# Low parts of the queries on 128 rows instead of 64, in the scores of three attentions

## Chip, core and metric

One Trainium2 chip, one NeuronCore. The metric is the device time of one execution in microseconds, as the median of the runs. Of the engines, TensorE (PE in the profile) multiplies matrices and loads their weights (PEld), VectorE (DVE) and ScalarE (ACT) read its results from PSUM, GpSimd (POOL) works on SBUF, and SyncE (SP) issues most DMAs.

## What is computed

A block of two layers: an input projection, four attentions side by side, a gated merge of their outputs, an output projection, and a mixture of 16 experts. The change touches the scores of three attentions: one with a sliding window and shared key heads (`win`), one that subtracts two softmaxes (`dif`), and one over a neighbourhood (`nat`). In all three, 64 numbers per head are multiplied; the fourth (`mla`) has 96.

```
def dense_attention(q, k, v):
    scale = q.shape[-1] ** -0.5

    def block(qb):
        logits = jnp.einsum('bqhd,bkhd->bhqk', qb, k).astype(jnp.float32) * scale
        p = jax.nn.softmax(logits, axis=-1)
        return jnp.einsum('bhqk,bkhd->bqhd', p.astype(v.dtype), v)
...
def trunk_layer(...):
    ys = [
        window_attention(wq, wk, wv, wkc, wvc, win_sink),
        dif_out(diff_attention(dq, jnp.concatenate([dkc, dk], axis=1), jnp.concatenate([dvc, dv], axis=1), lam)),
        neighbourhood_attention(nq, nk, nv, nkc, nvc, nat_rpb),
        flat_heads(dense_attention(mq, jnp.concatenate([mkc, mk], axis=1), jnp.concatenate([mvc, mv], axis=1))),
    ]
```

256 tokens and 256 context tokens make four tiles of 128. In layer 0 all four tiles are queries, in layer 1 only the first two.

## The kernel before

Products that need full precision are made of two fp32r parts each: a high part (`whi`, `hT[0]`) and what is left, a low part (`wlo`, `hT[1]`). A projection then takes three products (`mm3`, lines 284 to 288: high by high, high by low, low by high); ACT makes each high part and DVE the low part of the streamed weights (`parts`, lines 273 to 275).

**Scores.** A unit is a pair of heads and a tile of 128 queries. A head has 64 numbers, so a pair fills the 128 rows of a tile of queries or keys. The keys of a head i are kept in one 128-row tile: the high part on the head's own 64 rows, the low part on the other head's rows (`qk_post`, line 761). `heads` (line 911) makes the query side: `qs[i]` has the query's high part on both halves of the rows, so one 128-row product gives high by high plus high by low. ACT copies it (line 917), POOL repeats it on the other half (`QX`, recorded at line 261), and POOL subtracts to get the low part (line 919), which stands on the head's own 64 rows of one tile `ql` that both heads share. The second product of a head takes only these 64 rows of `ql` and of the keys. So a unit has four score products: two with 128 rows and two with 64. All are issued in `softmax2` (line 773), into the score banks `S0` and `S1`, which have one buffer each; with 512 columns for the first two query tiles and 256 for the others. Behind them come on DVE the maximum (line 782), on ACT the exponential (line 787), on POOL the normalization (line 261, `pp`), on TensorE the transposes (line 281), and the product with V (lines 827, 870).

**Tiles.** `qp` (line 765) takes the next of three buffers (`BUFS["qp"]`) of four 128x128 quarters: `qs[0]`, `qs[1]`, `ql`, and one that is unused. Every unit takes a new one. The `mla` attention takes its query parts from the same buffers, all four quarters.

**Order.** Within a layer the stages run one after the other (`run_main`): the projections of one attention go as main steps, and the units of the attention before as `side` items between them; so `win` runs beside the projections for `dif`, `dif` beside a merge, `mla` beside another, `nat` beside the merge of `mla`. `drain` ends each stage. The program is written in that order, and a scheduler with its own estimate of times sets the sequence of PE, DVE, ACT and POOL from it; SP's DMAs keep the written order. In the trace `win` stands at 97 to 225 us and 1233 to 1291, `dif` at 229 to 338 and 1318 to 1376, `nat` at 588 to 696 and 1544 to 1610. Then come the output projection and the experts, whose weights are streamed from about 700 to 1230 us and from 1612 us on.

Of the kernel before, what the change touches and what calls it, by code (L numbers as in the profile page):

```python
# [210 lines left out]
def kernel(ctx: ExitStack, tc: tile.TileContext, a, out, dbg=None, depth=L):  # L211
# [470 lines left out]
    def attention_layer(l, T, hT):  # L682
# [225 lines left out]
                act(nats[key, t], ps, AF.Copy)  # L908
            return f

        def heads(q, k):

            *qs, ql, _ = qp()
            rows = [slice(i * 64, (i + 1) * 64) for i in range(2)]
            for i in range(2):
                r, x = rows[i], rows[1 - i]
                act(qs[i][r], q[r], AF.Copy)  # L917
                QX(qs[i][x], qs[i][r])
                G.tensor_tensor(ql[r], q[r], qs[i][r], op=OP.subtract)
            return [[(i, qs[i], k[i], True, False) for i in range(2)],  # L920
                    [(i, ql[rows[i]], k[i][rows[i]], False, True) for i in range(2)]]

        def stage_win():
            w = {}
            idl = ids["wkv"]

            def ev_kv(t, ps):
                if "V" not in w:
                    kvt = b8r("wkv")
                    w["V"] = gp.tile([P, 512], F32, name="wV", tag="wV").rearrange("p (t n) -> p t n", t=4)  # L930
                    w["kT"] = [kvt[:, 0:512], kvt[:, 512:1024]]
                nats["wk", t] = t2("nat")
                act(nats["wk", t][:, :P], ps[:, :P], AF.Copy)
                V.tensor_copy(w["V"][:, t, :], ps[:, P:2 * P])
                if t == 3:
                    posts.extend(qk_post({t: nats["wk", t] for t in AT}, AT, 2, "wkn", *w["kT"]))

            def kv(t):

                ps = acc()  # L940
                tok = slice(t * P, (t + 1) * P)
                for n in range(KT):
                    mm3(ps[:, :256], (hT[0][:, n, tok], hT[1][:, n, tok]), ws.hl(*idl[n], ahead=t == 3), n == 0, n == KT - 1)
                ev_kv(t, ps)

            def ev_q(t, ps):
                n = t2("nat")
                act(n.rearrange("p (c s d) -> p s c d", c=4, s=2), ps.rearrange("p (s c d) -> p s c d", c=4, s=2), AF.Copy)
                nats["wq", t] = n
                if t == QT[-1]:  # L950
                    w["qT"] = b8("wqT")
                    posts.extend(qk_post({t: nats["wq", t] for t in QT}, QT, 8, "wqn", w["qT"]))
            steps = steps0(ev_kv, ev_q) if l == 0 else [lambda t=t: kv(t) for t in AT] + proj_steps("wq", 512, QT, ev_q)

            def slots():
                def ops(pi, tok, ks):
                    return heads(w["qT"].rearrange("p (b n) -> p b n", b=4)[:, pi, tok], [v[:, ks] for v in w["kT"]])
                return std_slots(ops, lambda b, pi, i: w["V"][:, b, i * 64:(i + 1) * 64], y_of(0), range(4), sink=True, mask=True)
            return steps, slots

        def stage_qkv(pre, gq, gk, br):
# [19 lines left out]

            def ops(pi, tok, ks):
                return heads(w["qT"].rearrange("p (b n) -> p b n", b=4)[:, pi, tok],
                             [v.rearrange("p (b n) -> p b n", b=4)[:, pi, ks] for v in w["kT"]])
            if br == 1:
                return steps, lambda: dif_slots(ops, w["V"], y_of(1))
            bias_t = {}

            def bias_load(pi):
# [14 lines left out]
                return r  # L1004

            def slots():
                bias_load(0)
                return std_slots(ops, lambda b, pi, i: w["V"][:, b, (2 * pi + i) * 64:(2 * pi + i + 1) * 64], y_of(2), range(4), bias=bias)
            return steps, slots
# [1182 lines left out]
```

## Time and profile before

| | |
|---|---|
| median of 3 runs | 1977.82 us (1973.92 to 1977.86) |
| profiled execution | 1979.95 us |
| its span in the trace | 1977.9 us |
| granted TensorE clock, mean | 0.957 of full speed |
| busy: PE, DVE, ACT, POOL | 92%, 61%, 51%, 37% |

An engine's busy time is no measure of how well it is used: products are pipelined, so that each is drawn longer than the distance to the next. What a product costs is read from the distance between starts in the order of time. A row of the order of time gives start, length, engine, line, operation, output and inputs, and then the shape of the weights (rows*columns) and of the moving data; in square brackets stands how long the engine was idle before and what ended that. Neighbours of one kind are merged under "xcount", and then the first one's shape is shown. "issue" means that nothing that the profile shows was waited for.

### The profile page before, as it was taken

To read this page: it belongs to the slowest core of one execution; us is meant where nothing else is said; L and a number is where in the kernel's file an instruction comes from. 1 tells how busy PE (TensorE), PEld (TensorE's weight loads), DVE (VectorE), ACT (ScalarE), POOL (GpSimd) and SP (SyncE) were. 2 spreads that over 40 slices of the span, in tenths; PEclk is the share of its full clock that TensorE was granted. 3 is DMA by queue.
4 is the path that set the end of the run, shared out by engine and by line. 5 is a ranking of instruction groups with operands and counts; after the bars stand their busy time and mean duration, and the time that the engine had idled before them with its cause. 6 is when DMAs were issued, how large, how long until landed. Compare 5 with 4: busy or idle time off the path is not lost. (4 is left out here: it accounts for less than half of the span.)

```text
span 1977.9 us, 26705 instructions
## 1 busy us (share of the span) xinstructions
PE 1825.4 (92%) x8748; PEld 1252.3 (63%) x8748; DVE 1215.9 (61%) x2314; ACT 1010.0 (51%) x2201; POOL 725.6 (37%) x1066
## 2 busy tenths in 40 slices
PE   7989999999999999849998959999999999699998
PEld 5846678777666678635554538566877667555563
DVE  4657566566555545765564456766668777656664
ACT  4436465554545534436555435655545655555451
POOL 0657353444535510352222234643336630111110
PEclk9989999999999999969999969899999999799999
DMA  9331052211481245648999855336422365379995
GB/s 341 130 138 33 27 179 64 62 54 51 174 316 56 75 162 207 226 169 305 390 395 396 348 211 208 129 123 233 126 69 89 107 212 215 129 303 419 420 400 243
DMA packets 120875, 392.39 MB, mean 198 GB/s; under 512 B 12652, under 2 KB 30348, under 8 KB 93968
## 3 DMA queue, kind: packets, MB, share of 16 engines
q1 hardware_dynamic: 114832, 377.36, 52.2%
q0 software_dynamic: 3424, 8.08, 1.2%
q10 hardware_dynamic: 2464, 5.08, 0.7%
q8 instruction: 73, 1.20, 0.2%
q14 instruction: 82, 0.67, 0.1%
HBM read 379.19 MB, written 15.27 MB: 199 GB/s over the span
## 5 line engine op out<-in xcount | busy, mean ns | idle before, releaser
L287 PE MATMUL acc<-wlo,hT 128*128 128x512 f32 (+2 forms) x976 | 384.7, 394 | 1.8 <-DVE wlo L275 1.8
L288 PE MATMUL acc<-whi,hT 128*128 128x512 f32 (+2 forms) x976 | 378.7, 390 | 0.2 <-DVE hT L275 0.2
L286 PE MATMUL acc<-whi,hT 128*128 128x512 f32 (+2 forms) x976 | 363.9, 398 | 2.3 <-ACT nat L1016 1.1
L274 ACT ACTIVATE whi<-raw 128x512 fp32r<-128x512 f32 (+1 forms) x376 | 231.5, 625 | 250.6 <-PE acc L288 184.1
L275 DVE TENSOR_TENSOR wlo<-raw,whi 128x512 fp32r<-128x512 f32 (+1 forms) x376 | 274.9, 742 | 137.2 <-ACT whi L274 135.7
L312 DVE TENSOR_TENSOR wlo<-raw,whi 128x512 fp32r<-128x512 f32 x256 | 189.6, 784 | 79.8 <-ACT whi L308 79.4
L308 ACT ACTIVATE whi<-raw 128x512 fp32r<-128x512 f32 x304 | 182.1, 628 | 80.1 <-PE h L288 43.2
L286 PEld LDWEIGHTS acc<-whi,hT 128*128 128x128 f32 x976 | 182.4, 188 | 56.0 <-issue 11.5
L287 PEld LDWEIGHTS acc<-wlo,hT 128*128 128x128 f32 x976 | 183.9, 188 | 46.0 <-issue 8.7
L288 PEld LDWEIGHTS acc<-whi,hT 128*128 128x128 f32 x976 | 183.5, 188 | 39.4 <-issue 5.8
L261 POOL TENSOR_SCALAR pp<-pp,sml 128x512 f32<-128x512 f32 (+1 forms) x168 | 120.0, 723 | 145.2 <-DVE sml L792 89.6
L787 ACT ACTIVATE pp<-S,sml 128x512 f32<-128x512 f32 (+1 forms) x192 | 117.3, 613 | 87.5 <-DVE sml L782 56.3
L310 POOL TENSOR_TENSOR wlo<-raw,whi 128x512 fp32r<-128x512 f32 x48 | 63.4, 1322 | 242.2 <-ACT whi L308 173.2
L782 DVE TENSOR_REDUCE sml<-S 128x1 f32<-128x512 f32 (+1 forms) x192 | 113.0, 597 | 43.6 <-PE S L773 41.9
L619 POOL TENSOR_TENSOR sml<-sml,nhalf 128x1 f32<-128x1 f32 (+3 forms) x110 | 122.7, 1117 | 7.0
L1966 PE MATMUL hh<-raw,xh 128*64 128x512 f32 x344 | 115.4, 614 | 5.0 <-DMA raw<-in_moe_w_dram 5.0
L287 PE MATMUL h<-wlo,xe 128*128 128x512 f32 x256 | 106.6, 416 | 2.1 <-POOL wlo L310 0.8
L618 POOL TENSOR_SCALAR sml<-sml 128x1 f32<-128x1 f32 (+3 forms) x110 | 37.5, 340 | 189.0 <-DVE sml L713 111.4
L281 PE MATMUL T<-cst,pp 128*128 128x128 f32 x560 | 92.2, 288 | 12.5 <-POOL pp L261 8.9
L286 PE MATMUL h<-whi,xe 128*128 128x512 f32 x256 | 100.3, 399 | 1.6 <-PEq L1612 1.6
L288 PE MATMUL h<-whi,xe 128*128 128x512 f32 x256 | 101.3, 396 | 0.0
L261 POOL TENSOR_SCALAR qp<-qp 64x128 fp32r<-64x128 f32 x144 | 53.4, 371 | 120.8 <-ACT qp L917 103.5
(440 smaller groups left out, 3449.7 us busy)
## 6 DMA issues: line engine op xcount, KB each, us to landing
raw<-in_moe_w_dram SPq DMA_DIRECT2D x133, 1024.0 KB
raw<-in_w_in_dram SPq DMA_DIRECT2D x124, 512.0 KB
raw<-in_ada_w_dram SPq DMA_DIRECT2D x48, 1024.0 KB
w<-in_moe_w_dram SPq DMA_DIRECT2D x36, 1024.0 KB
w<-in_moe_w_dram SPq DMA_DIRECT2D x60, 256.0 KB
raw<-in_w_branch_dram SPq DMA_DIRECT2D x24, 512.0 KB
raw<-in_w_out_dram SPq DMA_DIRECT2D x24, 512.0 KB
w<-in_moe_w_dram SPq DMA_DIRECT2D x16, 512.0 KB
```

Source lines behind the costliest of these rows:

```text
L261: G.tensor_scalar(o, i, s, s2, op0=OP.mult, op1=OP.mult)
L274: act(hi, src, AF.Copy)
L275: V.tensor_tensor(lo, src, hi, op=OP.subtract)
L286: mm(o, s[0], whl[0], start=start, stop=False)
L287: mm(o, s[0], whl[1], start=False, stop=False)
L288: mm(o, s[1], whl[0], start=False, stop=stop)
L308: act(hi, raw, AF.Copy)
L312: V.tensor_tensor(lo, raw, hi, op=OP.subtract)
L619: G.tensor_tensor(r, r, nhalf[:, :n], op=OP.pow)
L782: V.tensor_reduce(nm[:, i:i + 1], ps[i][:, :nk], axis=AX.X, op=OP.max, negate=True)
L787: act(p[:, :nk], ps[i][:, :nk], AF.Exp, bias=nm[:, i:i + 1], accum_out=nm[:, 2 + i:3 + i])
L1966: mm(hh[r:r + 64], x, wm.cols(pi, kk * 512, 512), start=k == 0, stop=k == KT - 1, tile_position=(0, r))
```

## The change

The unused fourth quarter of a query tile becomes a second low tile, so that each head has one. `padded` is called once at the start of each of the three attentions; it takes the three buffers and lets DVE write zeros (a constant times 0) on those rows of the two low tiles that belong to the other head. `heads` takes the three in turn for the units; POOL writes a low part on its own 64 rows, and the other rows stay zero. The second product of each head then takes all 128 rows of its low tile and of the keys: the zeros meet the keys' low part. The lines of the products in `softmax2` are the same.

```
+        def padded():
+
+            ring = [qp() for _ in range(BUFS["qp"])]
+            for v in ring:
+                for i in range(2):
+                    V.tensor_scalar(v[2 + i][64 - i * 64:128 - i * 64], C("ident")[64 - i * 64:128 - i * 64], 0.0, None, op0=OP.mult)
+            return ring
+
+        def heads(q, k, ring):
+
+
+            *qs, l0, l1 = ring[0]
+            ring.append(ring.pop(0))
+            ql = (l0, l1)
             for i in range(2):
-                r, x = rows[i], rows[1 - i]
+                r, x = slice(i * 64, i * 64 + 64), slice(64 - i * 64, 128 - i * 64)
                 act(qs[i][r], q[r], AF.Copy)
                 QX(qs[i][x], qs[i][r])
-                G.tensor_tensor(ql[r], q[r], qs[i][r], op=OP.subtract)
-            return [[(i, qs[i], k[i], True, False) for i in range(2)],
-                    [(i, ql[rows[i]], k[i][rows[i]], False, True) for i in range(2)]]
+                G.tensor_tensor(ql[i][r], q[r], qs[i][r], op=OP.subtract)
+            return [[(i, v[i], k[i], g == 0, g == 1) for i in range(2)] for g, v in enumerate((qs, ql))]
...
             def slots():
+                ring = padded()
+
                 def ops(pi, tok, ks):
...
             if br == 1:
-                return steps, lambda: dif_slots(ops, w["V"], y_of(1))
+                def dif():
+                    w["ring"] = padded()
+                    return dif_slots(ops, w["V"], y_of(1))
+                return steps, dif
...
             def slots():
+                w["ring"] = padded()
                 bias_load(0)
```

How the built programs stand: TensorE, ACT and POOL have as many instructions as before, DVE has 36 more. On TensorE, the first score of `nat` in layer 0 (beside the merge of `mla`) stood so before; `x2` is a head's high and low product, `hT` the projections' input, and L539 belongs to another small product:

```order
L286 MATMUL acc<-whi,hT 128x512
L287 MATMUL acc<-wlo,hT 128x512
L288 MATMUL acc<-whi,hT 128x512
L773 MATMUL S_5896<-nkT,qp 128x512 x2
L539 MATMUL S_5598<-raw,cs_89 32x512 x4
L286 MATMUL acc<-whi,hT 128x512
L287 MATMUL acc<-wlo,hT 128x512
```

and stands so now:

```order
L288 MATMUL acc<-whi,hT 128x512
L539 MATMUL S_5584<-raw,cs_89 32x512 x4
L773 MATMUL S_5890<-nkT,qp 128x512 x2
L286 MATMUL acc<-whi,hT 128x512
L287 MATMUL acc<-wlo,hT 128x512
L288 MATMUL acc<-whi,hT 128x512
```

A head's two products are still one behind the other between the products of the merge; only the small product beside them has changed sides.

On DVE, where `dif` begins in layer 0 (L782, L785, L790 and L792 belong to the softmax of the last `win` units, L275 splits streamed weights), it was before:

```order
L790 TENSOR_TENSOR sml<-sml 128x1
L782 TENSOR_REDUCE sml<-S_2166 128x1
L785 TENSOR_TENSOR sml<-sml,nsink 128x1
L790 TENSOR_TENSOR sml<-sml 128x1
L792 RECIPROCAL sml<-sml 128x2
L275 TENSOR_TENSOR wlo<-raw,whi 128x512 x2
L782 TENSOR_REDUCE sml<-S_2299 128x1
```

and is now, with the fills of two of the three query tiles (the first tile's stand some rows earlier):

```order
L782 TENSOR_REDUCE sml<-S_2087 128x1
L916 TENSOR_SCALAR qp<-cst 64x128 x2
L785 TENSOR_TENSOR sml<-sml,nsink 128x1 x2
L275 TENSOR_TENSOR wlo<-raw,whi 128x512
...
L782 TENSOR_REDUCE sml<-S_2159 128x1
L785 TENSOR_TENSOR sml<-sml,nsink 128x1
L916 TENSOR_SCALAR qp<-cst 64x128 x2
L785 TENSOR_TENSOR sml<-sml,nsink 128x1
L790 TENSOR_TENSOR sml<-sml 128x1
```

The fills (L916) stand two at a time between the last softmaxes of `win`, each behind a reduction of a `win` score.

## Rows read from the trace of the kernel before

**Rows 1.** The page: busy time of each engine.
```profile
PE 1825.4 (92%) x8748; PEld 1252.3 (63%) x8748; DVE 1215.9 (61%) x2314; ACT 1010.0 (51%) x2201; POOL 725.6 (37%) x1066
```

**Rows 2.** Busy by stretch: from:to, length, engines (instructions), clock, DMA, GB/s; seven summed.
```profile
125.00:167.00 42.00, 30.20 (x118) 17.45 (x119) 31.32 (x86) 28.77 (x86) 32.98 (x56) 0.72 0.05 15
...
1230.00:1253.00 23.00, 18.64 (x69) 10.93 (x71) 12.21 (x34) 14.63 (x39) 14.05 (x32) 0.78 0.01 2
1253.00:1293.00 40.00, 40.00 (x219) 24.09 (x212) 34.56 (x71) 21.92 (x53) 30.08 (x33) 1.00 0.50 184
...
sum 490.00, PE 483.64 PEld 325.63 DVE 310.60 ACT 257.28 POOL 243.94; mean PE 69.09 PEld 46.52 DVE 44.37 ACT 36.75 POOL 34.85
...
900.00:1230.00 330.00, 296.33 (x1370) 186.49 (x1369) 184.76 (x285) 174.05 (x327) 95.17 (x90) 0.93 0.85 328
```

**Rows 3.** Line 773: one attention's products, TensorE's idle time; products (x) by stretch.
```profile
L773 PE MATMUL S<-nkT,qp x96: 277/477/505, 588.4 to 1609.7; 128*128 128x512 f32 x32, 64*128 64x512 f32 x32, 128*128 128x256 f32 x16, 64*128 64x256 f32 x16
...
  issue: 38.1, 121
...
125.00:167.00 42.00, 15.69 (x32) 7.44 (x32) 0.72 0.05 15
...
227.00:340.00 113.00, 24.16 (x64) 12.03 (x64) 0.97 0.34 105
...
1230.00:1253.00 23.00, 9.46 (x16) 3.79 (x16) 0.78 0.01 2
```

**Rows 4.** Order of time, TensorE and its weight loader, around low products.
```profile
595.04 0.40 PE L286 MATMUL acc<-whi,hT 128*128 128x512 f32 x1
...
595.27 0.82 PE L773 MATMUL S<-nkT,qp 128*128 128x512 f32 x2
...
595.60 0.18 PEld L773 LDWEIGHTS S<-nkT,qp 64*128 64x128 f32 x1 [0.37 <-issue]
...
596.03 0.19 PEld L287 LDWEIGHTS acc<-wlo,hT 128*128 128x128 f32 x1 [0.24 <-issue]
...
596.36 0.40 PE L288 MATMUL acc<-whi,hT 128*128 128x512 f32 x1
...
607.01 0.59 PE L773 MATMUL S<-nkT,qp 128*128 128x256 f32 x2
...
607.86 0.39 PE L286 MATMUL acc<-whi,hT 128*128 128x512 f32 x1
...
622.71 0.91 PE L773 MATMUL S<-nkT,qp 128*128 128x512 f32 x3
...
623.12 0.19 PEld L773 LDWEIGHTS S<-nkT,qp 64*128 64x128 f32 x2 [0.25 <-issue]
...
623.55 0.66 PE L281 MATMUL T<-cst,pp 128*128 128x128 f32 x4
...
1375.61 0.19 PEld L773 LDWEIGHTS S<-dkT,qp 64*128 64x128 f32 x2 [0.37 <-issue]
```

**Rows 5.** Order of time, products of the fourth attention with 96 rows.
```profile
413.27 1.35 PEld L773 LDWEIGHTS S<-mkT,qp 96*128 96x128 f32 x6
...
413.51 1.55 PE L773 MATMUL S<-mkT,qp 96*128 96x512 f32 x6
...
414.90 0.27 PE L281 MATMUL T<-cst,pp 128*128 128x128 f32 x1
```

**Rows 6.** TensorE's waits in 125 to 167 (us, times, longest); then one score there.
```profile
PE T L281 <- POOL pp L261: 7.2, 3, 3.9
...
144.20 1.50 PE L773 MATMUL S<-wkv,qp 128*128 128x512 f32 x2
...
145.62 0.69 PE L827 MATMUL T<-pT,wV 128*64 128x256 f32 x2
```

**Rows 7.** DVE groups: multiplications by a constant (busy us, mean ns).
```profile
L1884 DVE TENSOR_SCALAR OHe<-cst,rkq 128x128 fp32r<-128x128 f32 x8 | 2.1, 327 | 0.0
...
L659 DVE TENSOR_SCALAR sm<-sm 128x128 f32<-128x128 f32 x2 | 0.5, 241 | 0.0
```

More of the change, by code (lines that the diff above doesn't have):

```diff
@@ L909, in nat_evac @@
             return f
-        def heads(q, k):
-            *qs, ql, _ = qp()
-            rows = [slice(i * 64, (i + 1) * 64) for i in range(2)]
+        def padded():
[8 more added lines that the diff above has]
+            ql = (l0, l1)
             for i in range(2):
-                r, x = rows[i], rows[1 - i]
+                r, x = slice(i * 64, i * 64 + 64), slice(64 - i * 64, 128 - i * 64)
                 act(qs[i][r], q[r], AF.Copy)
                 QX(qs[i][x], qs[i][r])
-                G.tensor_tensor(ql[r], q[r], qs[i][r], op=OP.subtract)
-            return [[(i, qs[i], k[i], True, False) for i in range(2)],
-                    [(i, ql[rows[i]], k[i][rows[i]], False, True) for i in range(2)]]
+                G.tensor_tensor(ql[i][r], q[r], qs[i][r], op=OP.subtract)
+            return [[(i, v[i], k[i], g == 0, g == 1) for i in range(2)] for g, v in enumerate((qs, ql))]
         def stage_win():
@@ L955, in slots @@
             def slots():
+                ring = padded()
                 def ops(pi, tok, ks):
-                    return heads(w["qT"].rearrange("p (b n) -> p b n", b=4)[:, pi, tok], [v[:, ks] for v in w["kT"]])
+                    return heads(w["qT"].rearrange("p (b n) -> p b n", b=4)[:, pi, tok], [v[:, ks] for v in w["kT"]], ring)
                 return std_slots(ops, lambda b, pi, i: w["V"][:, b, i * 64:(i + 1) * 64], y_of(0), range(4), sink=True, mask=True)
@@ L983, in ops @@
                 return heads(w["qT"].rearrange("p (b n) -> p b n", b=4)[:, pi, tok],
-                             [v.rearrange("p (b n) -> p b n", b=4)[:, pi, ks] for v in w["kT"]])
+                             [v.rearrange("p (b n) -> p b n", b=4)[:, pi, ks] for v in w["kT"]], w["ring"])
             if br == 1:
-                return steps, lambda: dif_slots(ops, w["V"], y_of(1))
+                def dif():
+                    w["ring"] = padded()
+                    return dif_slots(ops, w["V"], y_of(1))
+                return steps, dif
             bias_t = {}
```

## The prediction

> **What bounds the kernel now.** I read the page first, then busy time by stretch, then the score products of line 773 by stretch, and last single products in the order of time. On the page TensorE is busy 92% of the span, the next engine, DVE, 61% [rows 1]; these are averages over stages with different limits, so the stretches must tell. The three changed attentions stand in nine stretches. In seven of them (95 to 125, 167 to 227, 227 to 340, 585 to 700, 1253 to 1293, 1316 to 1378 and 1542 to 1612 us) TensorE is busy 483.6 of 490 us in sum, DVE 63% of it, ACT 53% and POOL 50%, and the closest that another engine comes is DVE with 86% in 1253 to 1293 [rows 2]. There TensorE sets the time. In the other two, 125 to 167 and 1230 to 1253, it is busy 48.8 of 65 us, at a mean granted clock of 0.72 and 0.78 (a part of the time at 1.2 GHz, not 2.4) [rows 2], and waits for POOL and ACT of the softmax [rows 6].
>
> The three attentions hold 288 score products in 72 units of four, half of them with 64 rows: 32 of each kind with 512 columns and 16 with 256 in `nat`, and as many in the other two. TensorE sat idle before line 773 for 38.1 us in 121 places until "issue", that is, behind nothing that the profile shows [rows 3]. The order of time shows where.
>
> **What a 64-row product costs.** Take the score at 595.27 us: the high product starts at 595.27, the weights of the product after the low one are taken at 596.03, and the product behind that starts at 596.36. That is 1.09 us from the first to the fourth start; 128-row products follow each other by 0.23 us (595.04, 595.27), so three take 0.69: 0.40 us too much. The weight loader shows why: it takes 128-row weights while the product before still runs, but stood 0.37 us before it took the 64-row weights, and 0.24 us before it took 128-row ones again [rows 4]. With 256 columns, 607.01 to 607.86 is 0.85 us, where 0.12 + 0.12 + 0.23 = 0.47 would do: 0.38 too much (0.12 is an estimate: half of 0.23 for half the columns) [rows 4]. That the rows make it, not the change between high and low parts nor the buffers, shows in a fourth attention that the change leaves alone: six 96-row products with weights from the same buffers stand between 128-row ones and take 413.51 to 414.90, 0.23 each, without a stop of the loader [rows 5]. I take **0.39 us** for a low product that stands alone.
>
> **The change, part by part.** (a) The 144 low products get 128 rows; their number, columns and sums stay. By the 96-row rows, each then costs its ordinary 0.23 or 0.12 us. 120 of them stand in the seven stretches and 24, half of 32 and 16, in the two others [rows 3]. In eight units, all in the seven stretches, both low products stand together; the first of these with 512 columns is at 623.12, the last at 1375.61. There they start as one, and three products take 622.71 to 623.55, 0.84 us instead of 0.69; a part of that comes from the transposes on either side, and I take 0.1 [rows 4]. So 104 x 0.39 + 8 x 0.1 = **41.4 us of TensorE time** where it sets the time. How much of it reaches the end: a unit's softmax on ACT, DVE and POOL gets up to 11% less time under it (in 227 to 340, 32 low products, 12.5 of 113 us) [rows 3]. TensorE's waits in these stretches are 6.4 us in all now, so the others deliver on time; DVE at 63% has room, at 86% little, but that is 40 of the 490 us [rows 2]. I take 90%, 37.3 us; the ends are half, 20.7, and all of it.
>
> (b) In the two starved stretches a low product is dearer: at 144.20 a high and a low one take 1.42 us at the lower clock, against 0.76 (595.27 to 596.03) at the higher [rows 4, 6], so the surplus lies between 0.39 and twice that. 24 x 0.39 to 0.78 = 9.4 to 18.7 us; I take 14. TensorE waits there for POOL and ACT, which wait for scores in turn, since each of the two score banks has one buffer: a part of the product's time is in that circle. I take half, **7 us**, between 0 and 14.
>
> (c) The zeros: 36 DVE fills of 64x128, six at each of six attention starts. No such form is in the trace; a 128x128 multiplication by a constant took 241 ns, one with fp32r output 327 ns [rows 7]: 8.7 to 11.8 us of DVE in all, at most 2 at a place. In the order they stand two at a time between reductions and the `wlo` splits that feed the projections; DVE's idle third hides them. A fill waits for the release of its buffer, but in the order its last reader comes before the reduction just ahead on DVE. I deduct **1 us**; uncovered it is 11.8.
>
> (d) The ring: before, each unit took the next of three tiles; now the same three are kept through an attention. The depth is the same, and a write waits for the readers of its quarter instead of the whole tile's. POOL and ACT run as many instructions as before. I cost this at nothing.
>
> (e) The scheduler's order: most of TensorE's sequence is the same; in layer 0 the second attention's scores and the last of the first's are mixed otherwise. No work is added; I give it nothing, and 5 us either way in the range.
>
> Sum: 37.3 + 7 - 1 = 43 us from the profiled execution's 1979.95 us, 1937. That execution is 2.1 us over the median of the runs, 1977.82, so I forecast **1935 us**. What follows the attentions moves with them: the expert weights, where DMA is at 85% between 900 and 1230 us [rows 2], are issued when the attention stages are drained, and so start earlier by as much.
>
> **The rivals.** *All of it comes back* (7%): both kinds of stretches in full, 41.4 + 14 = 55 us, 1922 us. For it, that TensorE waits so little now; against it, the waits on POOL and ACT in 125 to 167.
>
> *The softmax takes the place* (12%): with TensorE faster, transposes wait for POOL's normalized scores in the seven stretches too, as in 125 to 167, where three such waits took 7.2 us [rows 6]. Half of (a) and nothing of (b): 20 us, 1958. Against it: POOL and ACT have half of these stretches idle [rows 2].
>
> *Slower, by the fills* (3%): a fill holds DVE until the attention before has let go of its buffer, and with it the splits behind. A unit of `dif` takes 113 / 16 = 7.1 us (227 to 340); two units' wait at each of the four starts that follow another attention would be 57 us, 14 more than the gain: 1991. It turns the sign from 11 us a place. Against it: the place of the fills in the order, behind work that already needs those readers.
>
> *Slower, by lost concurrency* (2%): two 64-row products on different halves of the rows can run at the same time, and the eight units with both together show it. If every unit ran its two low products in the time of one, at no other price, 128 rows would add one product to each: 48 x 0.23 + 24 x 0.12 = 14 us [rows 3], 1992 us. It decides where low products stand together and the return is free; but 64 units have them apart, and even together three products take 0.84 us instead of 0.69 [rows 4]. The Trainium skill (TensorE: Matmul & The Clock Gate, Part 3 on packing small matmuls) speaks for this rival: a product with few rows takes as long as a full one, and pays when it is put beside another on distinct row groups, since they run together. By that rule the change loses the 14 us; the trace agrees on the common start, in eight units, and not on the price of one that stands alone.
>
> *It does not do what it says* (4%): the loader's stop comes from something else in these products and remains at 128 rows. Then only the fills are added: 1978 to 1981. Against it speak the 96-row products.
>
> **How the numbers follow.** The forecast has 72%, with a range of its own from 1924 (all of (a), 14 of (b)) to 1951 (two thirds of (a), none of (b)). The whole range, 1916 to 1960, takes in the first rival with the 5 us of (e) and the middle of the second; the second's far end, the slower ones and the last are left out, some 14%. A measurement of this kernel can tell about 0.2%, 4 us, from no change: faster has 72 + 7 + 12 = 91%, within it the last rival's 4%, slower 5%.
>
> **What would show it.** In the profile of the changed kernel: no 64-row form at line 773; idle time there until "issue" down from 38.1 us to a few; a score's products 0.23 us apart in 585 to 700; that attention (115 us now) shorter by 9 to 12 us. If the second rival holds, TensorE's share in the seven stretches falls, with waits on POOL or ACT `pp` before transposes. The forecast fails if low products of 128 rows still take over 0.3 us, if DVE waits some us before a fill, or if the expert stages end when they did before.

## The result, and the profile after

The changed kernel takes 1946.72 us (median of 4 runs, 1945.53 to 1947.77), the kernel before 1977.84 beside it: a ratio of 0.9842, with a 95% interval from 0.9829 to 0.9855. That is 31 us less where 43 were forecast. The profiled execution took 1947.77 us with a span of 1945.7; before, 1979.95 and 1977.9.

The page's line of busy times, in the form of [rows 1]:

```profile
PE 1782.1 (92%) x8748; PEld 1249.5 (64%) x8748; DVE 1224.5 (63%) x2350; ACT 1006.2 (52%) x2201; POOL 734.3 (38%) x1066
```

TensorE runs as many products as before, in 43.3 us less busy time. The share is 92% in both: it is still the engine that sets the time. DVE has 36 instructions more, the fills with zeros, and 8.6 us more busy time.

The products of line 773 for the third attention, with the idle time before that line, in the form of [rows 3]:

```profile
L773 PE MATMUL S<-nkT,qp x96: 278/393/505, 573.0 to 1574.2; 128*128 128x512 f32 x64, 128*128 128x256 f32 x32
...
  issue: 4.0, 7
```

No 64-row form is left, the median product went from 477 to 393 ns, and the stop behind "issue" went from 38.1 us in 121 places to 4.0 in 7. The heading of [rows 3] and the prediction call those 38.1 us TensorE's idle time; asked for each engine alone, the trace gives all of them to the weight loader (PEld) and none to the products. One score in the order of time (start, length, engine, line, operation), to be held against [rows 4]:

```profile
578.31 0.40 PE L286 MATMUL acc<-whi,hT 128*128 128x512 f32 x1
578.55 0.62 PE L773 MATMUL S<-nkT,qp 128*128 128x512 f32 x2
579.01 0.40 PE L287 MATMUL acc<-wlo,hT 128*128 128x512 f32 x1
579.25 0.39 PE L288 MATMUL acc<-whi,hT 128*128 128x512 f32 x1
```

The high and the low product and the next one behind them now take 0.70 us (578.55 to 579.25), 0.23 each, where three such starts took 1.09.

To see where the time went I cut both executions at the same products of the projections, so that each stretch holds the same work. In order: window and second attention of layer 0; the fourth attention; the third; the expert stage of layer 0; window, second, and fourth with third attention of layer 1; the last expert stage. Columns are from:to, length, busy time of TensorE, its loader, DVE, ACT and POOL (instructions), granted clock, DMA share, GB/s. First the kernel before:

```profile
114.10:335.10 221.00, 206.28 (x939) 144.33 (x938) 144.73 (x357) 125.23 (x352) 122.46 (x214) 0.92 0.24 73
335.10:564.20 229.10, 222.50 (x1124) 163.47 (x1123) 139.62 (x266) 115.36 (x284) 107.15 (x160) 1.00 0.32 108
590.10:697.70 107.60, 106.31 (x497) 73.62 (x493) 60.05 (x118) 54.41 (x139) 54.64 (x88) 1.00 0.22 64
800.40:1188.50 388.10, 322.07 (x1500) 198.47 (x1498) 222.37 (x374) 190.67 (x342) 122.65 (x132) 0.89 0.81 307
1215.60:1292.40 76.80, 72.44 (x349) 46.41 (x347) 56.92 (x119) 43.03 (x106) 52.84 (x72) 0.93 0.26 97
1315.80:1382.60 66.80, 66.80 (x327) 40.57 (x326) 41.87 (x89) 37.55 (x95) 27.16 (x50) 1.00 0.58 200
1510.90:1620.30 109.40, 105.09 (x511) 74.69 (x510) 85.52 (x144) 64.87 (x149) 61.45 (x83) 1.00 0.38 119
1676.70:1945.80 269.10, 243.39 (x1061) 146.32 (x1059) 165.48 (x285) 144.15 (x251) 43.94 (x37) 0.95 0.83 336
```

The changed kernel, the same stretches:

```profile
112.50:316.80 204.30, 184.93 (x939) 141.24 (x939) 144.17 (x361) 122.14 (x351) 121.92 (x210) 0.93 0.25 79
316.80:547.80 231.00, 223.38 (x1125) 163.79 (x1124) 141.20 (x272) 115.55 (x284) 107.82 (x163) 1.00 0.32 107
573.50:670.40 96.90, 95.30 (x493) 73.16 (x492) 58.39 (x116) 53.15 (x139) 58.03 (x89) 1.00 0.25 71
773.10:1160.50 387.40, 321.88 (x1500) 197.34 (x1498) 224.57 (x380) 191.41 (x342) 123.55 (x132) 0.90 0.81 307
1187.60:1263.40 75.80, 69.87 (x350) 46.72 (x348) 59.28 (x124) 42.72 (x106) 54.99 (x72) 0.95 0.27 98
1286.60:1349.10 62.50, 62.50 (x329) 41.41 (x328) 42.49 (x89) 37.25 (x95) 27.51 (x50) 1.00 0.67 213
1477.80:1584.50 106.70, 100.60 (x512) 75.01 (x510) 86.83 (x149) 64.68 (x149) 61.95 (x83) 1.00 0.39 120
1640.90:1912.80 271.90, 245.09 (x1060) 146.79 (x1060) 165.58 (x285) 144.23 (x251) 43.79 (x37) 0.94 0.82 333
```

The five stretches with the changed products became shorter by 16.7, 10.7, 1.0, 4.3 and 2.7 us, 35.4 in sum. Against that stand 1.9 more in the fourth attention, which the change does not touch, and 2.1 more in the two expert stages together. Where TensorE had hardly any idle time before, in the third attention of layer 0 and the second of layer 1, it has hardly any after (1.3 to 1.6 us, and none in both). In the others its idle time (length less busy time) grew: from 14.7 to 19.4 us in the first stretch, from 4.4 to 5.9 in the window attention of layer 1, from 4.3 to 6.1 in the stretch with the third attention of layer 1. Each table is one execution, and the stretches with a clock under 1.00 vary more than the others; the experiments show by how much.

### The profile page after: what moved, and what is told of

Same layout as the page of the kernel before. It is cut to its first block, busy times and chain, and to the rows that moved or that the text cites. A ratio compares the mean times of both kernels' runs of the same rounds, so it can differ in the third digit from the quotient of the medians.

```text
span 1945.7 us, 26785 instructions
## 1 busy us (share of the span) xinstructions
PE 1782.1 (92%) x8748; PEld 1249.5 (64%) x8748; DVE 1224.5 (63%) x2350; ACT 1006.2 (52%) x2201; POOL 734.3 (38%) x1066
## 5 line engine op out<-in xcount | busy, mean ns | idle before, releaser
L275 DVE TENSOR_TENSOR wlo<-raw,whi 128x512 fp32r<-128x512 f32 (+1 forms) x376 | 272.4, 735 | 132.5 <-ACT whi L274 128.3
L782 DVE TENSOR_REDUCE sml<-S 128x1 f32<-128x512 f32 (+1 forms) x192 | 111.6, 595 | 31.1 <-PE S L773 30.0
L281 PEld LDWEIGHTS T<-cst,pp 128*128 128x128 f32 x560 | 68.5, 145 | 39.2 <-POOL pp L261 12.8
```

The lines of the kernel that those rows point to most:

```text
L275: V.tensor_tensor(lo, src, hi, op=OP.subtract)
L281: tp(pt[:, k * P:(k + 1) * P], src[:, kt * P:(kt + 1) * P], ident)
```

## The experiments

My theory going in: a product of 64 rows between full-height ones costs some 0.39 us in all, for the stop of the weight loader on the way there and back. The change pays by taking that away and by nothing else. The rivals were the other tiles and the other order (the ring), the two heads' low products at the same time, and, for the missing 12 us, the softmax.

### The ring and its order alone

The changed kernel's ring and its two low tiles, without zeros, and with the low products on 64 rows:

```diff
-            for v in ring:
-                for i in range(2):
-                    V.tensor_scalar(v[2 + i][64 - i * 64:128 - i * 64], C("ident")[64 - i * 64:128 - i * 64], 0.0, None, op0=OP.mult)
...
-            return [[(i, v[i], k[i], g == 0, g == 1) for i in range(2)] for g, v in enumerate((qs, ql))]
+            rows = [slice(i * 64, (i + 1) * 64) for i in range(2)]
+            return [[(i, qs[i], k[i], True, False) for i in range(2)],
+                    [(i, ql[i][rows[i]], k[i][rows[i]], False, True) for i in range(2)]]
```

> The changed kernel with its three kept tiles and a low tile per head, but without the fills, and with low products on 64 rows as before. My theory (the 64-row products themselves cost TensorE 0.39 us each when they stand alone): the gain is gone, 1978 us, between 1970 and 1984, and idle time before the scores until issue is near 38 us again. Rival (the gain comes from keeping the tiles, from finer waits, or from the new order): about as the changed kernel, 1943 to 1952 us.

Measured: 1979.6 us (1974.47 to 1987.68), the kernel before 1975.51 on the same chip; ratio 1.0029, from 1.0005 to 1.0054. The gain is gone, so tiles and order do not make it. If anything the ring costs a little. The loader's idle time before line 773 until "issue" is back, 34.7 us in 112 places. Three stretches of its trace are needed below: the window and second attention of layer 0, the fourth attention of layer 0, and the fourth with the third of layer 1:

```profile
113.90:326.20 212.30, 200.40 (x939) 141.71 (x938) 145.22 (x357) 122.98 (x351) 121.30 (x212) 0.94 0.24 76
326.20:555.30 229.10, 222.49 (x1124) 163.51 (x1123) 139.31 (x266) 115.11 (x284) 107.20 (x160) 1.00 0.32 109
1502.90:1617.60 114.70, 106.41 (x511) 75.63 (x510) 85.94 (x144) 65.03 (x149) 59.40 (x83) 0.99 0.40 125
```

The first is 8.7 us shorter than in the kernel before, with the same rows in every product. So a difference of that size in this stretch, read from one execution each, does not tell what the rows are worth there.

### The rows alone

The kernel before with one line changed: the low product takes all 128 rows of the low tile that both heads share. Each head then also gets the other head's low part times the low part of the keys. There are no zeros and no ring.

```diff
-                    [(i, ql[rows[i]], k[i][rows[i]], False, True) for i in range(2)]]
+                    [(i, ql, k[i], False, True) for i in range(2)]]
```

> The kernel before with one edit: the low product takes all 128 rows of the shared low tile and of the keys, with no zeros, no fills, no ring. On the other head's rows it adds the low part of the other head's query times the low part of the keys, a product of two remainders. My theory: as the changed kernel, 1946 us, between 1940 and 1952; if the fills cost the 1 us that I gave them, 1945. Rival (ring and order make the gain): 1972 to 1980 us.

Measured: 1944.21 us (1942.21 to 1948.55), ratio 0.9836, from 0.9818 to 0.9855. The row count alone brings all that the change brings. Its time is 2.5 us under the changed kernel's, but the two were timed apart and their intervals overlap; so it is not shown to be faster or slower, and it needs less code. Two of its stretches, the fourth attention of layer 0 and the fourth with the third of layer 1, differ from the changed kernel's by about 2 us:

```profile
321.20:550.10 228.90, 222.31 (x1125) 163.59 (x1125) 139.80 (x267) 115.28 (x284) 108.17 (x163) 1.00 0.32 108
...
1484.60:1589.30 104.70, 100.25 (x510) 74.84 (x509) 84.98 (x142) 64.80 (x149) 61.48 (x83) 1.00 0.38 121
```

In the changed kernel these took 231.0 and 106.7 us, here 228.9 and 104.7. In the fourth attention of layer 0 the extra time goes with the zeros: the kernel with the window attention taken back, which has them too, shows 231.0, and the ring without zeros 229.1. In the other stretch the ring is not cleared: the kernel with the window attention taken back shows 106.9, but the ring without zeros, on 64 rows, took 114.7 us where the kernel before took 109.4.

What a fill does shows in the changed kernel. The group of the fills (busy us, mean ns, idle before them):

```profile
L916 DVE TENSOR_SCALAR qp<-cst 64x128 fp32r<-64x128 f32 x36 | 10.8, 301 | 1.9 <-PE yh L2031 1.2
```

and the third attention's start in layer 1, DVE and then TensorE in the order of time:

```profile
1511.13 0.68 DVE L782 TENSOR_REDUCE sml<-S 128x1 f32<-128x512 f32 x1
1511.85 0.86 DVE L916 TENSOR_SCALAR qp<-cst 64x128 fp32r<-64x128 f32 x2
1512.63 0.68 DVE L271 COPY pT<-T 128x512 f32<-128x512 f32 x1
```

```profile
1511.06 0.73 PE L773 MATMUL S<-nkT,qp 128*128 128x512 f32 x2
1513.36 0.87 PE L827 MATMUL T<-pT,mV 128*64 128x256 f32 x6 [1.56 <-DVE pT L271]
```

Two fills of 0.86 us together stand just ahead of the copy of `pT`, and TensorE waits 1.56 us for that copy. The copy starts 0.78 us after the fills do, so their own length is half of the wait. The wait at this product, 1.1 to 1.6 us, stands in the four kernels here that fill zeros for the third attention, and in none of the other eight. At this place the fills are not hidden.

### Two low products together

If two 64-row products run at the same time, it may be better to keep them and put each pair together. Both kernels here hold the first low product until both high ones have been issued; the second differs from the first in the low product's rows, as in the experiment before.

```diff
...
+                for p in prods[0]:
+                    ins = prod(*p)
+                for p in prods[1]:
+                    with tc.issue_after(ins.ins):
+                        ins = prod(*p)
...
```

> The kernel before, with the four products of a unit kept together on TensorE: high, high, low, low, and both low ones with 64 rows, so that they can run at the same time in all 72 units. My theory, from the units that had them together: a unit loses 0.1 to 0.17 us instead of twice 0.39, so 7 to 12 us over all against the same order with 128 rows, most of it on the path: 5 to 12 us slower than that one, and well under the kernel before, 1950 to 1965 us. Rival (concurrency, by the rule on packing): 14 us less TensorE time than the same order with 128 rows, so 8 to 14 us faster than that one.

> The same order, high, high, low, low, with 128 rows in the low products (shared low tile, no zeros, as in the kernel with one edit). My theory: near the changed kernel, 1944 to 1956 us, since holding the first low product until the second score bank is free costs a little latency only; 5 to 12 us faster than its 64-row twin. Rival (concurrency): 8 to 14 us slower than the twin.

Measured: 1980.75 us (1978.72 to 1982.8) on 64 rows, ratio 1.0026, from 1.0017 to 1.0036; 1969.63 us (1968.16 to 1971.75) on 128 rows, ratio 0.9968, from 0.9958 to 0.9979. In this order the full height is 11.1 us faster, as the theory had it, and not 8 to 14 slower as the concurrency rival had it. In the trace on 64 rows, 70 of the 72 units have their two low products one behind the other. The size has a simple reading: 72 units at 0.15 us (0.84 less 0.69, [rows 4]) make 10.8. By that reading the two run together, which saves one product's 0.23 us of the 0.39, and 0.16 remain to be paid.

Their own times missed what I expected of them: they lie 16 and 14 us over the upper end, and the one on 128 rows 25 us over the rows alone in the old order. In the second attention of layer 1, where TensorE never idles, one part of it can be read. The stretch for the rows alone, then the pairs on 128 and on 64 rows:

```profile
1293.30:1355.80 62.50, 62.50 (x328) 41.43 (x327) 42.54 (x89) 37.36 (x95) 26.79 (x50) 1.00 0.63 213
```

```profile
1306.60:1373.20 66.60, 66.26 (x328) 41.66 (x327) 42.69 (x87) 36.72 (x94) 24.62 (x50) 1.00 0.59 200
```

```profile
1311.00:1378.90 67.90, 67.90 (x328) 40.26 (x327) 41.66 (x87) 36.78 (x94) 25.22 (x50) 1.00 0.57 196
```

The same number of products takes 4.1 us longer in the held order, at the same rows. Line 539 issues narrow products of 32 columns of weights, in groups. In the order of time of the pairs on 128 rows, groups stand like this:

```profile
1316.82 1.07 PE L539 MATMUL acc<-raw,cs 128*32 128x512 f32 x8
...
1326.32 1.04 PE L539 MATMUL acc<-raw,cs 128*32 128x512 f32 x2
```

A group of two takes as long as a group of eight. In the held order there are 14 groups in this stretch, for the rows alone 11: three more at about 1 us each are 3 of the 4.1. So the hold lets other work fall apart into smaller groups. The stretch of the two pairs gives the price again: 67.9 against 66.6 us, 1.3 for eight units, 0.16 each. The rest of the 25 us I did not follow; cut in the same way, the traces of the held and of the old order on 128 rows differ in all the stretches with changed attentions (8.1 and 6.5 us in layer 0; 1.5, 4.1 and 5.7 in layer 1).

### The window attention on 64 rows, and it alone on 128

The changed kernel with the window attention taken back, by a copy of the old function beside the new one:

```diff
-                ring = padded()
-
...
-                    return heads(w["qT"].rearrange("p (b n) -> p b n", b=4)[:, pi, tok], [v[:, ks] for v in w["kT"]], ring)
+                    return heads64(w["qT"].rearrange("p (b n) -> p b n", b=4)[:, pi, tok], [v[:, ks] for v in w["kT"]])
```

> The changed kernel with one stage taken back: the 48 low products of the window attention (32 in layer 0, 16 in layer 1) use 64 rows again and carry no zeros; the other two attentions keep 128 rows. What it tells: what the window attention's share of the gain is. The prediction's own sum for these 48 (7 us in the two starved stretches, and 24 products at 90% of 0.39 us or less outside them) would make this kernel 13 to 15 us slower than the changed kernel, 1959 to 1962 us. My theory, from the stages of the two traces: the window attention waits for its softmax chain, so most of what its products save turns into waiting there. In layer 1 that stretch became 1.0 us shorter and no more; in layer 0 the window attention and the one after it became 16.7 us shorter together, of which some 11 belong to the 32 products of the other (as the third attention got 10.6 for its own 32). That leaves 5 or 6 plus 1: 1951 to 1955 us, 5 to 8 slower than the changed kernel. A rival, that the window attention brings nothing at all: 1946 to 1949.

Measured: 1953.28 us (1949.91 to 1956.25), ratio 0.9889, from 0.9865 to 0.9912. That is 6.6 us over the changed kernel, inside the 5 to 8 of the theory. The two were timed apart; held each against the kernel before timed beside it, the gains are 31.1 and 22.7 us, 8.4 apart. The counterpart is the kernel before with all rows in the window attention alone:

```diff
...
-                    [(i, ql[rows[i]], k[i][rows[i]], False, True) for i in range(2)]]
+                    [(i, ql, k[i], False, True) if full else (i, ql[rows[i]], k[i][rows[i]], False, True) for i in range(2)]]
```

> The kernel before with one edit, in the window attention alone: its 48 low products take all 128 rows of the shared low tile (so each head also gets the other head's low part times the low part of the keys); no zeros, no ring, and the other two attentions keep 64 rows. It is the counterpart of the kernel in which the window attention alone was taken back, without the ring of tiles. My theory says that the window attention is worth 5 to 8 us and not the 13 to 15 of the prediction's sum: 1967 to 1972 us where the kernel before takes 1975 to 1977. If the window attention were worth what the sum said, and the ring and the zeros had eaten it in the changed kernel: 1960 to 1963. If it is worth nothing: 1974 to 1978.

Measured: 1971.02 us (1969.63 to 1973.5), the kernel before 1976.14; ratio 0.9976, from 0.9965 to 0.9986, so 5.1 us, from 2.8 to 6.9. From both sides the window attention is worth 5 to 8 us, about half of what the prediction's sum gave it, and it is so without the ring too. In which layer it comes is not settled: against the kernel before, the second kernel is 5.9 us shorter in the first stretch (215.1 us) and 0.7 in the window attention of layer 1 (76.1); the first kernel is 1.1 longer than the changed one in the first stretch (205.4) and 4.2 in the other (80.0).

### A switch put where none was

The change cannot tell whether the price belongs to its three attentions or to any switch of row counts. In the fourth attention all products have 96 rows, and none stops the loader [rows 5]. Here its low products use 64 of them:

```diff
-                        r.append([(i, hi, k[0], True, False), (i, hi, k[1], False, False), (i, lo, k[0], False, True)])
+                        r.append([(i, hi, k[0], True, False), (i, hi, k[1], False, False), (i, lo[0:64], k[0][0:64], False, True)])
```

> The changed kernel with a switch of row counts added where neither kernel has one: the low product of each unit of the fourth attention uses 64 of its 96 rows (so 32 rows of 48 low products are left out of its scores), between products of 96 rows. The products become no longer and no shorter in columns; only the row count changes, three times in a unit of two banks. If the price is that of a switch from a full-height product to a 64-row one and back, it comes back here: 32 products over 512 columns at 0.39 us and 16 over 256 columns at 0.28 us make 17 us, and with the 72% that the change itself turned into time (31 of 43) 12: 1957 to 1966 us. If the price hung on something of the three attentions (their zero rows, which bank, the ring, the two heads' rows), this kernel is like the changed one, 1945 to 1949; and if fewer rows were cheaper in themselves, it is faster than 1944.

Measured: 1960.31 us (1959.73 to 1960.66), 13.6 over the changed kernel, inside 1957 to 1966. One unit of six products, TensorE in the order of time and then its loader:

```profile
382.42 2.23 PE L773 MATMUL S<-mkT,qp 96*128 96x512 f32 x6
384.58 0.64 PE L1098 MATMUL T<-cst,nat 128*96 128x128 f32 x4
```

```profile
383.07 0.18 PEld L773 LDWEIGHTS S<-mkT,qp 64*128 64x128 f32 x1 [0.37 <-issue]
383.50 0.30 PEld L773 LDWEIGHTS S<-mkT,qp 96*128 96x128 f32 x2 [0.25 <-ACT qp L1114]
384.16 0.18 PEld L773 LDWEIGHTS S<-mkT,qp 64*128 64x128 f32 x1 [0.36 <-POOL qp L1115]
384.58 0.39 PEld L1098 LDWEIGHTS T<-cst,nat 128*96 128x96 f32 x4 [0.24 <-DVE gt L1157]
```

Six products take 382.42 to 384.58, 2.16 us, where six of 96 rows took 1.39 [rows 5]: 0.77 more for two low products, **0.385 each**. The loader stands 0.37 and 0.25 us, the same two stops as in [rows 4]; the names behind the arrows are put down by the profile and mean little here, since the stops are alike in each case. The stretch between the second and the third attention of layer 1 holds eight such products, and TensorE sets the time there. The changed kernel and this one:

```profile
1349.10:1477.80 128.70, 124.67 (x604) 99.51 (x603) 88.62 (x172) 71.89 (x162) 59.52 (x80) 1.00 0.32 97
```

```profile
1360.90:1492.60 131.70, 127.67 (x603) 98.96 (x602) 88.89 (x173) 72.01 (x162) 59.16 (x80) 1.00 0.31 95
```

3.0 us for eight is 0.375 each. So the price is that of the switch, also in an attention that had none. The other two stretches with such products are less clean: the fourth attention of layer 0, with 32, became 12.1 us longer (243.1), but at a clock of 0.97 instead of 1.00, and the stretch with the third attention of layer 1, with eight and with DVE busy for 81% of it, only 0.3 (107.0 after 106.7).

### A lighter softmax

The missing 12 us: does the softmax take them? The first kernel is the kernel before, the second the changed one, and the third has the rows alone; all three leave out the sink, the bias and the multiplication of the probabilities in the window and the third attention.

```diff
-                pts, nm = softmax2(prods, nk, [pi, pi + 4] if sink else None,
-                                   bias(pi, t) if bias is not None and t < 2 else None, mk)
-                for i in range(2):
-                    pmul(pts[i][:, :nk], pts[i][:, :nk], nm[:, 6 + i:7 + i])
+                bias is not None and t < 2 and bias(pi, t)
+                pts, nm = softmax2(prods, nk, None, None, mk)
+                if not sink and bias is None:
+                    for i in range(2):
+                        pmul(pts[i][:, :nk], pts[i][:, :nk], nm[:, 6 + i:7 + i])
```

> The kernel before with a lighter softmax in the window and the third attention: the sink's operations, the bias addition and the multiplication of the probabilities by the reciprocal of their sum are left out there (so these two attentions compute something else); the low products keep 64 rows. It is the foot for its twin of 128 rows. TensorE waits 11.8 us in the window attention of layer 0 and 4.4 in that of layer 1; with a shorter chain I expect about half of that back, and little elsewhere: 1962 to 1974 us. Theory and rival differ over the twin, not over this one.

> The changed kernel with the same lighter softmax in the window and the third attention. What counts is the distance from its twin of 64 rows. My theory: the change brought 31 us and not 43 mostly because in the window attention (both layers) and in the third one of layer 1 the softmax chain and DVE's and GpSimd's work took the place of the switches; with that work gone the distance grows to 37 to 43 us, and the stages show it: the window and the second attention of layer 0 together shorter by 20 or more (16.7 with the full softmax), the window attention of layer 1 by 4 to 5 (1.0), the third attention of layer 1 by about 5 (2.8). The rival: the missing 12 us were never there (the price per product was read too high), or were lost to something else (the order, the filling of zeros, the clock): the distance stays 28 to 33 us.

> The kernel with the lighter softmax (sink, bias and the multiplication of the probabilities left out in the window and the third attention), and the low products on all 128 rows of the shared tile, without zeros or ring. Its foot is the light kernel of 64 rows (3267 us), its sister the light kernel made from the change (3232 us, 35.5 less). If softmax and ring together explain what was missing, the distance from the foot is 38 to 43 us: the window attention of layer 1 about 5 shorter as in the sister, the third attention of layer 1 4 to 5 shorter (2.0 in the sister, where the ring and the fills are), the third one of layer 0 10 to 11. If the ring and the fills cost nothing there, the distance is 33 to 36 and the third attention of layer 1 stays at 2 to 3.

Measured: 3267.34 us (3264.95 to 3271.5), 3231.83 (3228.7 to 3235.22) and 3235.48 (3231.98 to 3237.26). The absolute times missed the expectation by far: with other values in it the last expert stage takes some 650 us instead of 269. The distances are 35.5 and 31.9 us, which is neither the 37 to 43 of the theory nor clearly the rival's 28 to 33; the third kernel missed both of its own ranges, 38 to 43 and 33 to 36. The last expert stage differs between the three by as much as is in question (650.3, 651.8 and 655.2 us), and the products do not change there. So the stretches have to tell. The window and second attention of layer 0, the window attention of layer 1, and the fourth with the third of layer 1; first on 64 rows:

```profile
114.10:324.00 209.90, 200.37 (x939) 141.03 (x938) 132.14 (x293) 120.21 (x320) 102.23 (x182) 0.96 0.24 77
...
1205.20:1284.50 79.30, 75.87 (x349) 47.34 (x348) 55.77 (x96) 40.96 (x93) 45.70 (x60) 0.91 0.26 94
...
1502.70:1609.70 107.00, 104.81 (x513) 73.97 (x511) 81.97 (x127) 64.20 (x149) 47.56 (x67) 1.00 0.42 132
```

then made from the change:

```profile
114.30:306.50 192.20, 179.59 (x938) 138.75 (x937) 131.80 (x297) 117.08 (x319) 101.31 (x178) 0.97 0.26 83
...
1179.30:1253.50 74.20, 71.09 (x349) 47.19 (x349) 57.21 (x99) 40.16 (x91) 46.39 (x61) 0.95 0.27 100
...
1467.80:1572.80 105.00, 100.55 (x513) 74.70 (x510) 84.90 (x134) 65.18 (x150) 48.29 (x67) 1.00 0.40 129
```

and with the rows alone:

```profile
115.10:309.10 194.00, 179.66 (x938) 139.22 (x937) 130.92 (x291) 118.80 (x320) 101.17 (x180) 0.97 0.27 83
...
1179.50:1253.50 74.00, 70.02 (x345) 46.59 (x344) 53.71 (x93) 40.96 (x93) 45.71 (x60) 0.95 0.26 94
...
1468.30:1571.50 103.20, 100.74 (x514) 74.42 (x511) 80.19 (x127) 63.93 (x149) 48.18 (x67) 1.00 0.43 137
```

- The window attention of layer 1 gains 5.1 and 5.3 us instead of 1.0, as the theory wanted, and TensorE's idle time hardly grows (3.4 to 3.1 and 4.0; from 4.4 to 5.9 with the full softmax). But the theory is not shown by this. The light kernel on 64 rows is no shorter there (79.3 us, clock 0.91) than the two with the full softmax and 64 rows (76.8 at 0.93, 80.0 at 0.89); only the light ones on 128 rows are, 74.2 and 74.0 us against 75.7 to 76.1 in the changed kernel, the rows alone and the window attention alone. So the lighter softmax is worth 1.5 to 2 us there on 128 rows, and the rest of the 5 lies within what the 64-row kernels differ by.
- The third attention's stretch of layer 1 gains 2.0 with the zeros and 3.8 without them. A lighter softmax does not help it; leaving out the zeros and the ring does. Here the theory was wrong, and the experiment with the rows alone names the cause, zeros and ring taken together.
- The first stretch gains 17.7 and 15.9 us, not the 20 or more that the theory wanted, against 16.7 and 15.5 with the full softmax (the rows alone took 205.5 there). TensorE's idle time grows from 9.5 to 12.6 and 14.3. So the sink and the multiplication are not what takes the gain there.

## Why the prediction was right, and what it mis-sized

The time, 1946.72 us, lies in the range of 1916 to 1960 and in the forecast's own range of 1924 to 1951, 12 us above the forecast. Its mechanism is the one that the runs show: the switch to 64 rows and back. What was mis-sized is how much of it reaches the end. The prediction's own numbers, given to the stretches of the tables above by where its lone, paired and starved products stand, against what the two profiled executions show:

| stretch | predicted gain | measured |
|---|---|---|
| window and second attention, layer 0 | 15.8 + 4.7 | 16.7 |
| third attention, layer 0 | 9.0 | 10.7 |
| window attention, layer 1 | 1.6 + 2.3 | 1.0 |
| second attention, layer 1 | 4.4 | 4.3 |
| third (with fourth) attention, layer 1 | 5.6 | 2.7 |
| sum | 43.4 | 35.4 |

(The first number is 90% of 0.39 us for a lone product and 0.1 for a paired unit; the second is the starved products' share of 7 us, 16 of 24 in layer 0. In the first stretch 45 lone products make 0.9 x 45 x 0.39 = 15.8. Two lone products and a pair of layer 0 lie outside the stretches, so the sum is some 0.8 us under the prediction's 37.3 + 7.)

*Step (a), the price.* Right. [Rows 4] gave 0.39 us, a switch put into another attention cost 0.385 and 0.375, and the two stretches with hardly any idle time came out at 10.7 and 4.3 us for 9.0 and 4.4. The prediction's signs hold too: no 64-row form, "issue" at 4.0 us (the loader's, not TensorE's), 0.23 us a product, and the third attention of layer 0 shorter by 10.7 where 9 to 12 were named.

*Step (a), the 90%.* Right or low for the two stretches just named, and too high for one of layer 1: one share was taken for stretches that differ. The stretch of the fourth and third attention has DVE at 78% before (85.5 of 109.4 us) and gave 2.7 of 5.6; 4.7 come out without ring and zeros. The prediction had counted DVE's 86% only for 1253 to 1293.

*Step (b), the starved stretches.* This is where the sum was most too high. The window attention was given some 14 us in all (7 for its starved products, and 7 for 20 lone ones at 90% and two pairs); it is worth 5 to 8 by the timed experiments on it. Those change all its products at once, so they do not tell how much of the miss is the 7 and how much the 90%. Where TensorE waits for others, a faster product can end in a longer wait: its busy time in the first stretch fell by 21.4 us and its length by 16.7. What it waits for instead stays open. In layer 1 the softmax has a part of some 2 us. In layer 0 neither the sink nor the multiplication is it, and no one wait grew in every kernel: transposes behind POOL's `pp` took 7.2 us before, 6.4 in the changed kernel and 9.8 in the rows alone, scores behind ACT's `pp` 3.4, 4.9 and 4.2, products with V behind DVE's copy of `pT` none, 2.5 and 1.6. The length of that stretch is also no sure reading. The run with the switch in the fourth attention has the changed kernel's code up to that point, and took 4.3 us less for the same stretch, at 0.97 instead of 0.93:

```profile
114.60:314.60 200.00, 179.91 (x939) 138.10 (x938) 144.49 (x361) 121.94 (x351) 121.66 (x210) 0.97 0.25 79
```

So the same subtraction gives 16.7 or 21.0 us, and the prediction had 20.5; with the ring on 64 rows in place of the kernel before (212.3 us) it gives 8.0 or 12.3. That the sum was too high for the window attention rests on the times of whole runs, not on this stretch.

*Step (c), the fills.* Their size was right: 10.8 us of DVE for 36, against 8.7 to 11.8. The cover was not whole. The prediction let two at a time hide in DVE's idle third; in layer 1 two of them held up a copy that TensorE waited for, and the two stretches that differ from the rows alone lost 2.1 and 2.0 us, the second with the ring not told apart. Instead of 1 us, some 2 to 4 were lost there. The other attentions differ by at most 1.2 us, in both signs, and the whole times by 2.5, within their noise. By these estimates the window attention lacks 6 to 9 us of its 14 and the fills 1 to 3 beyond their 1, most of the 12 us between forecast and time.

*Steps (d) and (e), the ring and the order.* They were costed at nothing, with 5 us either way. The ring at 64 rows measured 0.05% to 0.54% slower, 1 to 11 us, so it costs a little; how much of that remains at 128 rows was not measured apart from the zeros.

*The rivals.* All of it, 55 us, did not come back. That the softmax takes the place is shown for no more than some 2 us, in the window attention of layer 1; the lighter softmax brought no more gain in the other stretches. Lost concurrency fell: even paired, the 64-row products are 11.1 us slower than full-height ones in the same order. The Trainium skill (TensorE: Matmul & The Clock Gate, Part 3 on packing small matmuls) has small products gain when they run together on distinct rows. The traces agree that they run together, and here it does not pay, since the way there and back costs 0.39 us and running together saves 0.23. The last rival, that the change does nothing, fell with the profile after; and the rival of the fills too: DVE's longest wait ahead of a fill did not reach 2 us (all of them together, 1.9), and of the 1.56 us that TensorE waited at one place, half came from the fills' own length.

## What to carry to other kernels

A product of 64 rows among products of 96 or 128 is not cheaper; alone among them it cost 0.39 us more here than it would at their height, so count the switches, not the rows, and look for the loader's idle time behind "issue". Of a saving on the busiest engine, price each stretch by its own idle time: where that engine already waits, take half or less (the window attention gave 5 to 8 us here, where 44 lone products at 0.39 us make 17). A shared operand whose extra rows add only a product of two remainders is simpler than rows of zeros, and leaves out the work of making them.

## What the runs showed of the hardware

- Around a lone 64-row product of 512 columns the loader stops for 0.37 us on the way into 64 rows and for 0.24 back, from 128 as from 96 rows ([rows 4] and 383.07 to 384.58 in the run with the added switch); ahead of the pair at 623.12 the stop into 64 rows is 0.25. Between 96 and 128 rows there is none [rows 5]. The Trainium skill (TensorEngine Tiling (Array Packing), Key Properties) states that a change of tiling mode drains TensorE. The trace agrees for 64 rows and gives the price; 96 rows beside 128 behave as one mode in it.
- Groups of two and of eight products with 32 columns of weights take 1.04 and 1.07 us. Where the held order has three such groups more, they add about a microsecond each, which I had not counted when I held products back.
- The same code took 4.3 us more or less in one stretch, with the granted clock at 0.93 or 0.97 (above), while in the second attention of layer 1, where TensorE hardly idles, the clock is 1.00, 2.4 GHz, in every trace here. In the window attention of layer 1, the kernel with that attention taken back took 80.0 us at 0.89 where the kernel before, with the same products there, took 76.8 at 0.93:

```profile
1189.40:1269.40 80.00, 75.63 (x350) 47.64 (x350) 57.43 (x125) 43.31 (x106) 52.89 (x72) 0.89 0.25 93
```

So a difference of a few us in one stretch means little unless two kernels or two measurements agree.
